# Reading the second up-projection tile of the first pair ahead of its convolution, and broadcasting the second norm's factors two steps of k sooner

## The chip, the cores and the metric

The kernel runs on one core of one Trainium2 chip. The metric is the device time of that core in microseconds. Its engines are TensorE (PE in the profile; PEld is its weight load), VectorE (DVE), ScalarE (ACT), GpSimd (POOL) and SyncE (SP), which here only issues DMAs.

## The reference

One inference step of a decoder layer, for a prompt group (1 x 512 tokens) and a sample group (8 sequences x 8 tokens) that share the weights. The kernel puts both side by side as 576 token columns. What matters here is the part behind the mixers:

```
x = x + concat(retention, attention) @ w_out          # 1024 x 1024
h = rmsnorm(x, norm2_w)                                # mean of squares over 1024, per token
ua, ub = split(h @ w_up, 2816)                         # 1024 x 5632
conv = conv_b + sum_j buf[:, j:j+T] * conv_w[j]        # buf: two saved rows, then ua; width 3
x = x + (silu(conv) * ub) @ w_down                     # 2816 x 1024
y = rmsnorm(x, normf_w)
```

Data are float32.

## The kernel before

**Tiling.** Activations lie transposed: features on the 128 partitions, the 576 tokens along the free axis. A *dense* tile is a [128 features x 576 tokens] product, accumulated in two PSUM banks as two halves of 288 columns (`d` tiles, from the pool `psd` with two buffers). Float32 precision is made of three products: each operand is split into a high part and a low part (rounded to float32r, and the remainder), and high x high, high x low, low x high are summed. One *step of k* is thus six matmuls of 288 columns, three weight parts by two halves; a tile over 1024 input features is eight steps. Weights come as raw blocks by SP (`wraw`, `wrawb`), ScalarE makes the high part (`whi`, line 289), VectorE the low part (`wlo`, line 296), half a block (four steps) at a time, some halves ahead of use.

**The feed-forward part.** The 2816 features are 22 blocks f of 128, in chunks f = 0..7, 8..15, 16..21; after each chunk comes its share of the down projection. For each f two results are needed, the branch that is convolved (`pa`) and the one that multiplies it (`pb`). The odd f, and f=0, make them as two dense tiles, one after the other (`up`, `up_post`). The even f from 2 on make both by a scheme with seven products instead of eight (`up_seven`, `post_seven`): a *slab* of 84 matmuls at line 1274 into banks `m`, whose weights and inputs are sums and differences of quarters (`ws`, and the tiles `T`, made in `out_post` from line 1213 on). The fourth quarter of a slab adds into the bank of the first, and so needs that bank's copy by ScalarE (line 1280) first.

**The norm.** The second norm's factor is a number per token. It is not multiplied into h; the up projection runs on the unscaled h, and the products are scaled as they are read out of PSUM, by `rstd_b`. `norm2` makes it: sums over the features by matmul (line 1159), a reciprocal root in small VectorE steps, and then `row_broadcast`, five transposes (line 415) which spread the factors over the partitions, and two copies (lines 416, 417). Nothing of f=0 can be read out before that.

**After the products of f=0** (`up_post`): line 1337 and 1338 read `pa` out into `ue` (scaled), ScalarE starts the convolution (line 1341), VectorE adds the two other taps (lines 1345, 1346), ScalarE takes the silu (line 1348), VectorE reads `pb` out as `g` (line 1353), multiplies both (`gated`, lines 1320, 1321), and ScalarE and VectorE split the result into `ghi` and `glo` (lines 1323, 1325), the inputs of the down projection.

**Order.** Every engine runs its own queue in the order in which the program issues it. A small planner, `Merge`, sets that order: each stage is a generator, and what it yields is an estimate in ns, first of the TensorE work just issued and then of the time until its next piece should be issued; `yield None` waits for a flag. TensorE's dense stream drives the planner's clock (738 per step of k). The numbers in the yields are thus due times that decide places in queues, not waits on the chip. A `d` tile takes over the buffer of an earlier one, and its first matmul waits for the last reader of that one.

Of the kernel before, what the change touches and what calls it, by code (L numbers as in the profile page):

```python
# [22 lines left out]
T = NP + NS  # L23
# [123 lines left out]
def decoder_step(ctx, tc, a):  # L147
    nc = tc.nc
    pe, dve, act, pool, sp = nc.tensor, nc.vector, nc.scalar, nc.gpsimd, nc.sync
# [208 lines left out]
    def tok(ps):  # L358
        return ps[:, C0:C0 + T]
# [27 lines left out]
    rstd_b = cst.tile([P, T], F32, name="rstd_b")  # L387
# [18 lines left out]
    def rstd_cols(dst, ss, n):  # L406
        dve.tensor_scalar(ss, ss, 1.0 / n, EPS, op0=OP.mult, op1=OP.add)
        rsqrt(dst, ss, stat[:, 35:40])

    def row_broadcast(dst, cols):  # L410
        p1, p2 = mtile(), mtile()
        for j in range(5):
            r, s = rows_of(j)
            ps = p1[:, s] if j < 4 else p2[:, :NS]
            pe.transpose(ps, cols[:r, j:j + 1].to_broadcast([r, P]), ident[:r, :r])
        dve.tensor_copy(dst[:, :NP], p1)
        dve.tensor_copy(dst[:, NP:], p2[:, :NS])
# [713 lines left out]
    def tmp(name):  # L1131
        return fp.tile([P, UE], F32, name=name, tag="tmp", bufs=6)
# [21 lines left out]
    def token_sums(dst, x):  # L1154
        dve.memset(dst, 1.0)
        ps = mtile()
        for j in range(5):
            r, s = rows_of(j)
            pe.matmul(ps[:r, j:j + 1], x[:, s], ones[:, 0:1], start=True, stop=True)
        dve.tensor_copy(dst[:, 0:4], ps[:, 0:4])  # L1160
        dve.tensor_copy(dst[:NS, 4:5], ps[:NS, 4:5])
# [14 lines left out]
    def norm2():  # L1176
        token_sums(ss2, acc)
        rstd_cols(stat[:, 20:25], ss2, D)
        yield 2200.0, 3700.0
        row_broadcast(rstd_b, stat[:, 20:25])  # L1180
        norm2_made.append(1)
        yield 550.0, 100.0
# [15 lines left out]
    def out_post(m, ps):  # L1198
# [15 lines left out]
        if last:  # L1214
            yield 0.0, 5000.0
            yield from norm2()
# [21 lines left out]
    def seqs(t, off, n):  # L1238
        return t[:, NP + 2:UE].rearrange("p (b t) -> p b t", b=B)[:, :, off:off + n]

    def by_seq(x):
        return x.rearrange("p (b t) -> p b t", b=B)

    def up(f, n, ghi, glo, made):
        if f in SEVEN:
            yield from up_seven(f, n, ghi, glo, made)
            return
        pa = dtile()
        yield from dense(pa, ("up", f), hhis, hlos, 0, KD, True, True, made=h_made)
        pb = dtile()  # L1250
        done = []
        mg.add(up_post(f, n, pa, pb, done, ghi, glo, made), None, 4000.0 if f == 0 else 0.0)
        yield from dense(pb, ("up", NF + f), hhis, hlos, 0, KD, True, True)
        done.append(1)
# [63 lines left out]
    def gated(f, n, g, c, ghi, glo, made):  # L1318

        dve.tensor_tensor(g[:, :NP], g[:, :NP], c[:, :NP], op=OP.mult)  # L1320
        dve.tensor_tensor(by_seq(g[:, NP:T]), by_seq(g[:, NP:T]), seqs(c, 0, TS), op=OP.mult)  # L1321
        yield 0.0, 1000.0
        act.copy(ghi[n], g[:, :T])  # L1323
        yield 0.0, 1500.0
        dve.tensor_sub(glo[n], g[:, :T], f32(ghi[n]))  # L1325
        made[n] = 1
        up_made.append(f)
        if f % 2 == 0:
            keep_rows()

    def up_post(f, n, pa, pb, done, ghi, glo, made):
        u = ues[f % 2]
        ya, L = tok(pa), UE - 2
        while not norm2_made or not cs_made:
            yield None
        pool.tensor_copy(seqs(u, 0, 2), by_seq(csT[:, f]))
        dve.tensor_mul(u[:, 2:NP + 2], ya[:, :NP], rstd_b[:, :NP])
        dve.tensor_mul(seqs(u, 2, TS), by_seq(ya[:, NP:]), by_seq(rstd_b[:, NP:]))  # L1338
        yield 0.0, 1800.0
        c = tmp("cv")  # L1340
        act.activation(c[:, :L], u[:, 0:L], AF.Identity, scale=convw[:, 0, f:f + 1], bias=convb[:, f:f + 1])
        pool.tensor_copy(cout[:, 0:2, f], u[:, NP:NP + 2])
        pool.tensor_copy(by_seq(cout[:, 2:, f]), seqs(u, TS, 2))
        yield 0.0, 1800.0
        dve.scalar_tensor_tensor(c[:, :L], u[:, 1:L + 1], convw[:, 1, f:f + 1], c[:, :L], op0=OP.mult, op1=OP.add)
        dve.scalar_tensor_tensor(c[:, :L], u[:, 2:L + 2], convw[:, 2, f:f + 1], c[:, :L], op0=OP.mult, op1=OP.add)
        yield 0.0, 1300.0
        act.activation(c[:, :L], c[:, :L], AF.Silu)
        while not done:
            yield None  # L1350
        yield 0.0, 1400.0
        g = tmp("g")
        dve.tensor_mul(g[:, :T], tok(pb), rstd_b)
        yield 0.0, 1000.0
        yield from gated(f, n, g, c, ghi, glo, made)

    def conv_state_out():
# [175 lines left out]
```

## Time and profile before

| | us |
|---|---|
| median of 3 runs | 824.35 |
| lowest and highest run | 824.2, 825.31 |
| profiled execution, own time | 825.07 |
| its span, first to last instruction | 823.3 |
| TensorE busy in the span | 796.0 (97%) |
| VectorE busy | 518.2 (63%) |
| ScalarE busy | 345.0 (42%) |
| mean granted clock of TensorE | 0.990 of full |

All the times in the rows further down are microseconds from the span's start; a row's second number is the length of the piece or instruction. `L341` is a line of the program, `d<-hhi,whi` says what is written from what, and brackets give the idle time of that engine just before, with what ended it. The second norm lies at 393 to 401 us, f=0 and f=1 up to 421, then slabs and dense pairs alternate up to 487, and the first chunk's down projection follows.

### The profile page before, as it was taken

To read this page: it belongs to the slowest core of one execution; us is meant where nothing else is said; L and a number is where in the kernel's file an instruction comes from. 1 tells how busy PE (TensorE), PEld (TensorE's weight loads), DVE (VectorE), ACT (ScalarE), POOL (GpSimd) and SP (SyncE) were. 2 spreads that over 40 slices of the span, in tenths; PEclk is the share of its full clock that TensorE was granted. 3 is DMA by queue.
4 is the path that set the end of the run, shared out by engine and by line. 5 is a ranking of instruction groups with operands and counts; after the bars stand their busy time and mean duration, and the time that the engine had idled before them with its cause. 6 is when DMAs were issued, how large, how long until landed. Compare 5 with 4: busy or idle time off the path is not lost.

```text
span 823.3 us, 16179 instructions
## 1 busy us (share of the span) xinstructions
PE 796.0 (97%) x6439; PEld 757.5 (92%) x6439; DVE 518.2 (63%) x1098; ACT 345.0 (42%) x691; POOL 99.0 (12%) x199
## 2 busy tenths in 40 slices
PE   7999999999999999999899999999999999999994
PEld 6999999887888888999799999999999999999994
DVE  5664555665646566787767875347878534778663
ACT  5423232454535567456334452124444312444522
POOL 1311202011110213022001100000110000110021
PEclk9999999999999999999989999999999999999997
DMA  9355653778887863427245554215545621544603
GB/s 268 110 171 140 191 178 96 187 208 220 224 246 207 224 172 103 122 87 251 77 153 180 180 179 152 79 53 179 180 135 174 205 77 52 180 136 147 214 1 115
DMA packets 179673, 128.68 MB, mean 156 GB/s; under 512 B 14849, under 2 KB 176273, under 8 KB 179086
## 3 DMA queue, kind: packets, MB, share of 16 engines
q1 hardware_dynamic: 178445, 93.75, 40.3%
q10 hardware_dynamic: 928, 33.63, 11.3%
q8 instruction: 51, 0.84, 0.4%
q0 software_dynamic: 224, 0.28, 0.1%
q14 instruction: 25, 0.20, 0.1%
HBM read 121.52 MB, written 39.66 MB: 196 GB/s over the span
## 4 chain that ended last, share of the span: by engine, by line
PE 83%; DVE 8%; ACT 3%; issue 3%; DMA 1%; POOL 0%; ACTq 0%; SPq 0%; DVEq 0%; POOLq 0%
PE d L341 52%; PE m L1274 11%; PE m L980 3%; PE d L546 2%; PE m L1025 2%; DVE wlo L296 1%; PE m L907 1%; PE d L990 1%; PE m L894 1%; PE m L593 1%; ACT whi L289 1%; PE px L505 1%; DVE blo L1325 1%; PE px L341 1%; PE m L763 1%
## 5 line engine op out<-in xcount | busy, mean ns | idle before, releaser
L341 PE MATMUL d<-bhi,whi 128*128 128x288 f32 x786 | 176.8, 306 | 2.9 <-ACT bhi L1323 1.7
L341 PE MATMUL d<-blo,whi 128*128 128x288 f32 x786 | 168.1, 295 | 0.8 <-DVE blo L1325 0.8
L341 PE MATMUL d<-bhi,wlo 128*128 128x288 f32 x786 | 168.1, 295 | 0.0
L341 PEld LDWEIGHTS d<-bhi,whi 128*128 128x128 f32 x786 | 124.6, 189 | 8.7 <-issue 3.1
L341 PEld LDWEIGHTS d<-blo,whi 128*128 128x128 f32 x786 | 126.0, 188 | 1.5 <-DVE blo L1325 1.5
L341 PEld LDWEIGHTS d<-bhi,wlo 128*128 128x128 f32 x786 | 126.2, 188 | 0.0
L296 DVE TENSOR_TENSOR wlo<-wraw,whi 128x512 fp32r<-128x512 f32 (+1 forms) x145 | 99.7, 705 | 39.5 <-ACT whi L289 39.3
L289 ACT ACTIVATE whi<-wraw 128x512 fp32r<-128x512 f32 (+1 forms) x145 | 87.3, 619 | 81.2 <-PE d L341 71.8
L341 PE MATMUL d<-hhi,whi 128*128 128x288 f32 x312 | 67.9, 299 | 4.4 <-DVE ue L1338 4.4
L341 PE MATMUL d<-hhi,wlo 128*128 128x288 f32 x312 | 67.7, 298 | 0.0
L341 PE MATMUL d<-hlo,whi 128*128 128x288 f32 x312 | 67.4, 298 | 0.0
L341 PEld LDWEIGHTS d<-hhi,whi 128*128 128x128 f32 x312 | 51.0, 192 | 4.9 <-issue 4.8
L341 PEld LDWEIGHTS d<-hlo,whi 128*128 128x128 f32 x312 | 50.8, 191 | 0.0
L341 PEld LDWEIGHTS d<-hhi,wlo 128*128 128x128 f32 x312 | 50.8, 191 | 0.0
L1274 PE MATMUL m<-T,whi 128*128 128x288 f32 x240 | 48.6, 295 | 0.0
L1389 DVE TENSOR_TENSOR xT<-d,xT 128x576 f32<-128x576 f32 x23 | 17.4, 757 | 40.7 <-PE d L341 40.7
L296 DVE TENSOR_TENSOR wlo<-wrawb,whi 128x512 fp32r<-128x512 f32 (+1 forms) x32 | 22.6, 713 | 28.7 <-ACT whi L289 28.7
L1274 PEld LDWEIGHTS m<-T,whi 128*128 128x128 f32 x240 | 38.4, 188 | 0.2 <-ACT ct L1280 0.2
L1274 PE MATMUL m<-T,wlo 128*128 128x288 f32 x120 | 35.5, 296 | 0.0
L1323 ACT CAST bhi<-g 128x576 fp32r<-128x576 f32 x22 | 14.8, 674 | 49.1 <-DVE g L1321 49.0
L888 POOL TENSOR_SCALAR s<-s,sc 128x128 f32<-128x128 f32 (+3 forms) x32 | 18.3, 579 | 140.4 <-DVE sc L886 125.8
L981 ACT COPY kt<-m 128x384 f32<-128x384 f32 x32 | 15.3, 478 | 39.3 <-PE m L980 37.2
(333 smaller groups left out, 1574.7 us busy)
## 6 DMA issues: line engine op xcount, KB each, us to landing
wraw<-in_w_up_dram SPq DMA_DIRECT2D x33, 512.0 KB, 3.7
wraw<-in_w_in_dram SPq DMA_DIRECT2D x26, 512.0 KB, 6.4
kc<-in_cache_win_k_dram SPq DMA_DIRECT2D x32, 256.0 KB, 3.5
vc<-in_cache_win_v_dram SPq DMA_DIRECT2D x32, 256.0 KB, 3.5
wraw<-in_w_down_dram SPq DMA_DIRECT2D x12, 512.0 KB, 3.5
wrawb<-in_w_up_dram SPq DMA_DIRECT2D x11, 512.0 KB
kc<-in_cache_win_k_dram SPq DMA_DIRECT2D x64, 64.0 KB, 3.3
vc<-in_cache_win_v_dram SPq DMA_DIRECT2D x64, 64.0 KB, 3.1
```

The costliest lines, as they stand in the source:

```text
L289: act.activation(split[j][0][:, :n], src, AF.Copy)
L296: dve.tensor_sub(split[j][1][:, :n], src, f32(split[j][0][:, :n]))
L341: pe.matmul(ps[:, C0 + s * H2:C0 + (s + 1) * H2], wt[:, x], b[k][:, s * H2:(s + 1) * H2], start=first and k == k0 and wt is hi and b is xh ...
L505: pe.transpose(ps[:, s], xn[:r, j, k * P:(k + 1) * P], ident[:r, :r])
L546: pe.matmul(ps[i][:, C0 + s * H2:C0 + (s + 1) * H2], wt[:, k % 4], x[k][:, s * H2:(s + 1) * H2], start=k == 0 and wt is hi and x is xhis, ...
L888: pool.tensor_scalar(s[:, :n], s[:, :n], c[:, 2:3], 1.0, op0=OP.mult, op1=OP.mult)
L980: pe.transpose(ps[:, j * P:(j + 1) * P], K[u, x][:, 3 * w + j], ident)
L981: (act.copy if w else dve.tensor_copy)(kt[:, w * 384:w * 384 + 384], ps[:, :384])
L1025: pe.matmul(ps[x * 32:(x + 1) * 32, :P], pt[:, j, x * 32:(x + 1) * 32], v, start=j == 0, stop=j == 6, tile_position=(0, x * 32))
L1274: pe.matmul(dst, wt[:, k], b[:, k], start=q in (0, 1, 2, 5) and k == 0 and wt is hi and b is xh, stop=k == 3 and wt is lo, skip_group_chec ...
L1323: act.copy(ghi[n], g[:, :T])
L1389: dve.tensor_add(xT[:, m], tok(ps), xT[:, m])
```

## The change

Two edits. In `norm2` the due time of the broadcast goes from 3700 to 2300 behind the small steps. In `up_post`, for f=0 alone, `g` is read out of `pb` before the two taps of the convolution on VectorE; this piece waits until all matmuls of `pb` are issued. For the other f nothing changes in the code.

```diff
     def norm2():
         token_sums(ss2, acc)
         rstd_cols(stat[:, 20:25], ss2, D)
-        yield 2200.0, 3700.0
+        yield 2200.0, 2300.0
         row_broadcast(rstd_b, stat[:, 20:25])
...
         pool.tensor_copy(by_seq(cout[:, 2:, f]), seqs(u, TS, 2))
+        g = None
+        if f == 0:
+            while not done:
+                yield None
+            yield 0.0, 500.0
+            g = tmp("g")
+            dve.tensor_mul(g[:, :T], tok(pb), rstd_b)
         yield 0.0, 1800.0
         dve.scalar_tensor_tensor(c[:, :L], u[:, 1:L + 1], convw[:, 1, f:f + 1], c[:, :L], op0=OP.mult, op1=OP.add)
...
         yield 0.0, 1400.0
-        g = tmp("g")
-        dve.tensor_mul(g[:, :T], tok(pb), rstd_b)
-        yield 0.0, 1000.0
+        if g is None:
+            g = tmp("g")
+            dve.tensor_mul(g[:, :T], tok(pb), rstd_b)
+            yield 0.0, 1000.0
         yield from gated(f, n, g, c, ghi, glo, made)
```

The lines behind the second edit get higher numbers in the changed kernel: 1345, 1346 and 1348 become 1352, 1353 and 1355, and the product g is line 1350 for f=0 and 1361 for the other dense f.

First place, TensorE's queue in the second tile of f=0 (`d_5123`), whose weights come as two halves (`whi_5026`, then `whi_5058`) of four steps each. Before:

```order
L341 MATMUL d_5123<-hhi_4457,wlo_5066 128x288 x2
L415 MATMUL m_5196<-ident_69,stat_74 128x128 x4
L415 MATMUL m_5197<-ident_69,stat_74 128x64
L341 MATMUL d_5123<-hhi_4457,whi_5058 128x288 x2
L341 MATMUL d_5123<-hlo_4458,whi_5058 128x288 x2
L341 MATMUL d_5123<-hhi_4457,wlo_5066 128x288 x2
L341 MATMUL d_5217<-hhi_4457,whi_5095 128x288 x2
```

And in the changed kernel, same queue and tile:

```order
L341 MATMUL d_5123<-hhi_4457,wlo_5034 128x288 x2
L341 MATMUL d_5123<-hhi_4457,whi_5058 128x288 x2
L341 MATMUL d_5123<-hlo_4458,whi_5058 128x288 x2
L341 MATMUL d_5123<-hhi_4457,wlo_5066 128x288 x2
L415 MATMUL m_5184<-ident_69,stat_74 128x128 x4
L415 MATMUL m_5185<-ident_69,stat_74 128x64
```

The transposes stood behind the third step of the second half, one step ahead of the first tile of f=1 (`d_5217`); now they stand behind its first step, three steps ahead.

Second place, TensorE's queue where the second tile of f=1 begins, with what its first matmul waits for. Before (`d_5217` and `d_5297` are the first and second tile of f=1):

```order
L341 MATMUL d_5217<-hhi_4457,wlob_5132 128x288 x2
L341 MATMUL d_5297<-hhi_4457,whi_5174 128x288 [waits DVE_49,PE_49,Activation_49]
L341 MATMUL d_5297<-hhi_4457,whi_5174 128x288
L341 MATMUL d_5297<-hlo_4458,whi_5174 128x288 x2
L341 MATMUL d_5297<-hhi_4457,wlo_5182 128x288 x2
```

In the changed kernel the two tiles are called `d_5225` and `d_5299`:

```order
L341 MATMUL d_5225<-hhi_4457,wlob_5132 128x288 x2
L341 MATMUL d_5299<-hhi_4457,whi_5174 128x288 [waits DVE_49,Activation_49]
L341 MATMUL d_5299<-hhi_4457,whi_5174 128x288
L341 MATMUL d_5299<-hlo_4458,whi_5174 128x288 x2
L341 MATMUL d_5299<-hhi_4457,wlo_5182 128x288 x2
```

The matmuls are the same; the first one's wait on TensorE itself (on the end of an earlier tile in the buffer that it takes over) is gone, a wait on VectorE and one on ScalarE stay.

Third place, the queues of VectorE and ScalarE from the T tiles to the convolution of f=1. On VectorE, the first piece of the difference (`ue_4467` belongs to f=0):

```order
 L1195 TENSOR_TENSOR T<-h,T 128x288
+L1350 TENSOR_TENSOR g<-d,rstd_b 128x576
+L1195 TENSOR_TENSOR T<-h,T 128x288
 L278 TENSOR_TENSOR ws<-ws,wraw 128x512
 L296 TENSOR_TENSOR wlo<-wraw,whi 128x512
-L1195 TENSOR_TENSOR T<-h,T 128x288
-L1345 SCALAR_TENSOR_TENSOR cv<-ue_4467,vec,cv 128x592
-L1346 SCALAR_TENSOR_TENSOR cv<-ue_4467,vec,cv 128x592
+L1352 SCALAR_TENSOR_TENSOR cv<-ue_4467,vec,cv 128x592
+L1353 SCALAR_TENSOR_TENSOR cv<-ue_4467,vec,cv 128x592
```

The read of g stood behind these rows; it now stands before the last T low half and before the convolution of f=0. A little further on the same queue (`ue_4469` belongs to f=1):

```order
 L1338 TENSOR_TENSOR ue_4469<-d,rstd_b 128x8x8
-L1353 TENSOR_TENSOR g<-d,rstd_b 128x576
 L1320 TENSOR_TENSOR g<-g,cv 128x512
 L1321 TENSOR_TENSOR g<-g,cv 128x64
 L270 TENSOR_TENSOR wraw<-wraw 128x512
 L296 TENSOR_TENSOR wlob<-wraw,whib 128x512
-L1345 SCALAR_TENSOR_TENSOR cv<-ue_4469,vec,cv 128x592
-L1346 SCALAR_TENSOR_TENSOR cv<-ue_4469,vec,cv 128x592
-L1325 TENSOR_TENSOR blo<-g,bhi 128x576
+L1325 TENSOR_TENSOR blo<-g,bhi 128x576
+L1352 SCALAR_TENSOR_TENSOR cv<-ue_4469,vec,cv 128x592
+L1353 SCALAR_TENSOR_TENSOR cv<-ue_4469,vec,cv 128x592
```

The low half of f=0's product (line 1325) has passed the convolution of f=1. ScalarE's queue over the same stretch, before:

```order
L289 ACTIVATE whi<-wrawb 128x512 x2
L1193 ACTIVATE T<-t 128x288 x2
L1341 ACTIVATE cv<-ue_4467,vec 128x592
L1193 ACTIVATE T<-h 128x288 x2
L289 ACTIVATE whi<-wraw 128x512
L1348 ACTIVATE cv<-cv 128x592
L289 ACTIVATE whi<-ws 128x512
L1341 ACTIVATE cv<-ue_4469,vec 128x592
L289 ACTIVATE whib<-wraw 128x512
L1323 CAST bhi<-g 128x576
```

And in the changed kernel:

```order
L289 ACTIVATE whi<-wrawb 128x512
L1193 ACTIVATE T<-t 128x288 x2
L1341 ACTIVATE cv<-ue_4467,vec 128x592
L289 ACTIVATE whi<-wrawb 128x512
L1193 ACTIVATE T<-h 128x288 x2
L289 ACTIVATE whi<-wraw 128x512
L1355 ACTIVATE cv<-cv 128x592
L289 ACTIVATE whi<-ws 128x512
L1323 CAST bhi<-g 128x576
L1341 ACTIVATE cv<-ue_4469,vec 128x592
L289 ACTIVATE whib<-wraw 128x512
```

One weight split has fallen behind the T tiles and the activation of f=0, and the cast of f=0's product (line 1323) has passed the activation of f=1 and the weight split behind it. The queues of GpSimd and SP hold the same instructions in the same order.

## Rows read from the trace of the kernel before

**Rows 1.** The waits of TensorE, 380 to 520: us in total, times, longest us.
```profile
PE d L341 <- DVE ue L1338: 4.4, 2, 3.9
```

**Rows 2.** Timeline of TensorE, 392 to 424: start, us, what, [idle before <-releaser].
```profile
399.47 0.80 PE L415 MATMUL m<-ident,stat 128*128 128x128 f32 x5
400.20 0.53 PE L341 MATMUL d<-hhi,whi 128*128 128x288 f32 x2
...
401.80 0.50 PE L341 MATMUL d<-hhi,whi 128*128 128x288 f32 x2 [0.55 <-DVE ue L1338]
...
412.26 0.82 PE L341 MATMUL d<-hhi,whi 128*128 128x288 f32 x2 [3.86 <-DVE ue L1338]
...
421.47 0.29 PE L1274 MATMUL m<-hhi,whi 128*128 128x288 f32 x1
```

**Rows 3.** Windows: length, busy by engine, granted clock, DMA share, GB/s.
```profile
225.00:235.00 10.00, 8.77 (x83) 8.12 (x85) 6.34 (x17) 5.16 (x12) 2.57 (x9) 1.00 0.83 255
412.30:418.20 5.90, 5.90 (x25) 5.90 (x26) 4.75 (x8) 2.21 (x4) 0.21 (x2) 0.50 0.93 325
432.00:445.00 13.00, 13.00 (x100) 13.00 (x99) 9.69 (x20) 6.14 (x11) 2.19 (x6) 1.00 0.51 161
```

**Rows 4.** Timeline of VectorE, 392 to 425.
```profile
396.97 0.17 DVE L400 SCALAR_TENSOR_TENSOR stat<-stat 128x5 f32<-128x5 f32 x1
...
400.11 0.69 DVE L416 COPY rstd_b<-m 128x512 f32<-128x512 f32 x1 [2.36 <-PE m L415]
...
405.76 0.46 DVE L1195 TENSOR_TENSOR T<-h,T 128x288 fp32r<-128x288 f32 x1 [0.57 <-ACT T L1193]
...
412.03 0.75 DVE L1353 TENSOR_TENSOR g<-d,rstd_b 128x576 f32<-128x576 f32 x1
...
415.62 0.83 DVE L1346 SCALAR_TENSOR_TENSOR cv<-ue,vec,cv 128x592 f32<-128x592 f32 x1
...
418.63 0.69 DVE L296 TENSOR_TENSOR wlo<-ws,whi 128x512 fp32r<-128x512 f32 x1 [1.51 <-ACT whi L289]
424.23 0.69 DVE L296 TENSOR_TENSOR wlo<-ws,whi 128x512 fp32r<-128x512 f32 x1 [4.90 <-ACT whi L289]
```

**Rows 5.** Timeline of ScalarE, 392 to 425.
```profile
402.90 0.87 ACT L1341 ACTIVATE cv<-ue,vec 128x592 f32<-128x592 f32 x1
...
417.97 0.63 ACT L289 ACTIVATE whi<-ws 128x512 fp32r<-128x512 f32 x1 [3.63 <-PE d L341]
...
423.26 0.40 ACT L1280 COPY ct<-m 128x288 f32<-128x288 f32 x1 [4.07 <-PE m L1274]
```

**Rows 6.** Timeline of VectorE at the convolutions of f=3, 5, 7, 11, 13.
```profile
444.84 0.69 DVE L296 TENSOR_TENSOR wlo<-wraw,whi 128x512 fp32r<-128x512 f32 x1 [1.44 <-ACT whi L289]
445.45 0.75 DVE L1325 TENSOR_TENSOR blo<-g,bhi 128x576 fp32r<-128x576 f32 x1
...
446.98 0.84 DVE L1346 SCALAR_TENSOR_TENSOR cv<-ue,vec,cv 128x592 f32<-128x592 f32 x1
...
471.83 0.84 DVE L1346 SCALAR_TENSOR_TENSOR cv<-ue,vec,cv 128x592 f32<-128x592 f32 x1
...
494.98 0.84 DVE L1346 SCALAR_TENSOR_TENSOR cv<-ue,vec,cv 128x592 f32<-128x592 f32 x1
...
594.98 0.83 DVE L1346 SCALAR_TENSOR_TENSOR cv<-ue,vec,cv 128x592 f32<-128x592 f32 x1
...
619.83 0.84 DVE L1346 SCALAR_TENSOR_TENSOR cv<-ue,vec,cv 128x592 f32<-128x592 f32 x1
```

**Rows 7.** Chain of waits, 470 to 505 and 545 to 630: start, us, what.
```profile
500.09 4.93 PE d L341 x35
...
545.54 11.14 PE m L1274 x84
556.68 12.70 PE d L341 x96
...
617.01 11.55 PE m L1274 x84
```

## Prediction

> **What bounds the kernel now.** I read three views for one question: where does TensorE stand still, and who lets it go on. The waits between 380 and 520 us name a single large one: matmuls of line 341 waited 4.4 us for VectorE's line 1338, in two pieces, the longer 3.9 us [rows 1]. The timeline of TensorE puts them at 401.80 and 412.26 us, each at the first matmul of a new d tile [rows 2]: first and second tile of f=1. A row calls line 1338 the releaser because the second tile of f=1 took over the buffer of the first tile of f=1, and had to wait until that tile was read. The windows add what the pause costs afterwards: in the 5.9 us behind it the granted clock was 0.50, the 1.2 GHz level, where other stretches show 1.00 [rows 3].
>
> The second thing to see is less plain. VectorE's conv step of the odd f (line 1346) ends the vector chain of a pair of f. It starts at 446.98 for f=3 and at 471.83 for f=5, and in the second chunk at 594.98 and 619.83: 24.85 us apart each time [rows 6]. TensorE's own period for such a pair is shorter: four slabs start between 545.54 and 617.01, so (617.01 - 545.54) / 3 = 23.82 us [rows 7]. So VectorE and ScalarE, handing work to each other, go round in 24.85 us by themselves, and TensorE gains about 1 us on them per pair. That shows in the slab at 617.01, which took 11.55 us where the one at 545.54 took 11.14 [rows 7]: there the lead of the vector side is used up. A busy TensorE in these stretches is no proof that it sets the time. The down projection of the first chunk starts at 500.09, only after the vector chain's last piece, 5.1 us after the conv of f=7 at 494.98 [rows 6, 7].
>
> From f=1 to f=3 the same conv step takes 446.98 - 415.62 = 31.36 us [rows 4, 6]: 6.51 more than 24.85. VectorE's idle rows there give 1.51 and 4.90, together 6.41 [rows 4]; both times for ScalarE, which itself sat idle 3.63 and 4.07 us for TensorE [rows 5]. This is how the pause at 412 reaches the end of the chunk.
>
> **The change, step by step.** Durations are from the profiled execution: span 823.3 us, own time 825.07, which is 0.72 above the median of the runs, 824.35. One step of k is six matmuls; 96 of them, a pair of tiles, take 12.70 us [rows 7], so a step takes 0.79 and a tile 6.35.
>
> *Transposes two steps sooner.* They stood at 399.47 [rows 2], and come to 399.47 - 1.59 = 397.88. Their input is ready: the last step on the factors starts at 396.97 and takes 0.17 [rows 4]. Line 416 follows at 400.11 - 1.59 = 398.52, and so does everything behind it on VectorE. The count of matmuls is the same; TensorE's wait at 401.80 goes, since the buffer's reader is now done by about 400.1 and TensorE arrives at about 401.0 (400.20 plus one step). Gain there 0.8.
>
> *g of f=0 read ahead.* The same product of 0.75 us [rows 4], neither added nor removed, now stands before the last of the T tiles' low halves and before the conv. On ScalarE one weight split (0.63) falls behind the activation of line 1341 (0.87) [rows 5]. Its end becomes 402.90 - 1.59 + 0.87 + 0.63 = 402.81; the vector queue would otherwise come to its low half about 0.5 us before. Bounds for this wait are 0 and 0.87; I take 0.5. The T low half that stood at 405.76 [rows 4] then starts at 405.76 - 1.59 + 0.5 = 404.67, and g ends 0.46 + 0.75 later, near 405.9. TensorE reaches the second tile of f=1 at 401.0 + 6.35 = 407.4. So 1.5 us are to spare, the tile starts without a wait, and with no pause the clock has no reason to fall. Before, the tile started at 412.26, 4.1 after 401.80 + 6.35; and it took until 421.47, 9.21 instead of 6.35 [rows 2]. TensorE therefore comes to the first slab at about 413.7: 0.8 + 4.1 + 2.9 = 7.7 us sooner.
>
> *What the vector side makes of it.* From line 416 to the conv step of f=1 it took 415.62 - 400.11 = 15.51 us. Three things are added. The 0.5 above. Then the low half of the product g (line 1325, 0.75), which now stands before f=1's conv and stood behind it. And the order ScalarE now has, in which cast and activation precede a weight split that VectorE wants: the same order stands before f=3's conv, and there VectorE sat idle 1.44 [rows 6]. Together 15.51 + 0.5 + 0.75 + 1.44 = 18.20, from 398.52: the conv of f=1 starts at 416.72, which is 1.1 us *later* than before. But the 6.51 us of waiting after it go, because TensorE, 7.7 sooner, is no longer what is waited for. f=3's conv comes to 416.72 + 24.85 = 441.57 instead of 446.98: 5.41 sooner. From there both kernels run the same instructions in the same order; f=5, f=7, and the down projection keep the 5.4.
>
> Seen from TensorE it is the same sum: 7.7 gained, then about 0.3 us given back in the first slab and 24.85 - 23.82 = 1.03 in each of the two others, where it now waits for the copy of its first product bank, which stands behind the odd f's silu on ScalarE: 5.3.
>
> The moved steps issue no DMA. SP's weight loads hang on VectorE's low halves and keep their order; none of VectorE's listed waits in this stretch of the trace is for a transfer, and I cost them at nothing. If that cover failed, the loads would come late in both kernels, at the same point of the vector chain.
>
> Sum: 825.07 - 5.4 = 819.7 for a profiled execution, and **819.0 us** against the median.
>
> **Rivals.**
>
> *All of the 7.7 us stay: 816.7.* For it: TensorE and its weight loads are busy 13.00 of 13 us in 432 to 445, VectorE 9.69 [rows 3]. The Trainium skill (Perfetto Trace Analysis, "Identifying the Most-Contended Engine") says that the engine with the highest occupancy is the one whose gaps are to be closed, TensorE being judged by its weight loads; by that rule the gap's whole 7.7 would come back. Against it stands the 24.85 us period, shown twice, against TensorE's 23.82.
>
> *The second tile of f=1 still takes the first one's buffer: 824.0.* Then the early read frees nothing. Its releaser is then still line 1338 of f=1, which comes 1.59 - 0.5 - 0.75 = 0.34 sooner, and pause and half clock remain. For it: the profile names line 1338 for both waits. Against it: the first matmul of that tile loses its wait on TensorE's own earlier tile in the changed order.
>
> *Slower: the clock falls at the slabs, 827.6.* TensorE will now stop for about 1 us in the slabs of f=4 and f=6 and for less in that of f=2. If such stops brought the granted clock to 0.50, each would cost what the one at 412 cost, 9.21 - 6.35 = 2.86; three make 8.6, and from the second on (5.7) the gain is gone. Against it: in 225 to 235 us TensorE was busy 8.77 of 10 us, at a clock of 1.00 [rows 3]. The Trainium skill (TensorE: Matmul & The Clock Gate, "A second HAM failure mode: psum-queue depth-cycling") tells of a kernel whose frequent short idles between matmul groups made the clock swing; this row does not bear it out here.
>
> **How the numbers follow.** Forecast 0.84, all of it 0.07, buffer kept 0.05, clock 0.02, something else that cancels it 0.02. A difference of 0.2% is 1.65 us, about what a measurement tells from none. Faster by more: the first two cases, 0.91. Within: the kept buffer and most of the rest, 0.06. Slower: 0.03. The range: at the low end the full 7.7 (816.7) is partly let in; at the high end the 1.51 us idle before 418.63 might not go, which leaves 3.9 (820.5), and the three runs of before lie up to 0.96 from their median. That makes 816.9 to 821.1.
>
> **What would show it.** Right: line 415 near 397.9; no idle of TensorE before either tile of f=1; no half clock near 412; first slab near 413.7; the conv of f=1 near 416.7, a little later than before; f=3's near 441.6; stops of about 1 us in the slabs of f=4 and f=6; down projection near 494.7. Wrong: a releaser "line 1338" before the second tile of f=1, a clock of 0.50 in a slab, or f=3's conv more than 26 us after f=1's.

## The result and the profile after

The changed kernel takes 820.06 us (median of five runs, 819.24 to 820.61), the kernel before on the same chip 824.97 (five runs, 824.20 to 825.45). The ratio is 0.9941, with an interval of 0.9927 to 0.9955: 4.9 us less, between 3.7 and 6.0. The forecast was 819.0, which meant 5.4 less. Its direction and its path held; one term was too large, and the kernels below show which.

The profiled execution of after took 820.61 us, its span 818.6. Before comparing times in two traces one has to line them up. The second norm's sums (line 1159) are the last thing on TensorE that the change can't touch, and they already differ. First before, then after, both the timeline of TensorE:

```profile
393.52 1.16 PE L1159 MATMUL m<-small,acc 128*128 128x1 f32 x10
```

```profile
394.79 1.16 PE L1159 MATMUL m<-small,acc 128*128 128x1 f32 x10
399.15 0.80 PE L415 MATMUL m<-ident,stat 128*128 128x128 f32 x5
402.36 0.43 PE L341 MATMUL d<-hhi,whi 128*128 128x288 f32 x2
408.73 0.42 PE L341 MATMUL d<-hhi,whi 128*128 128x288 f32 x2
415.07 0.29 PE L1274 MATMUL m<-hhi,whi 128*128 128x288 f32 x1
```

The profiled execution of after comes to that point 1.27 us later. The instructions up to there are the same, and the difference is there within the first 22 us of the span: the same matmuls of line 505 start at 20.02 us in before and at 21.38 in after. So 1.27 is taken off each time of after: line 415 at 397.88, the first slab at 413.80, where before had 399.47 and 421.47 [rows 2]. There is no idle time before either tile of f=1 (402.36 and 408.73), where before had 0.55 and 3.86 [rows 2]. The waits of TensorE between 380 and 520 us (us in total, times, longest) no longer name line 1338 [rows 1]:

```profile
PE m L1274 <- ACT ct L1280: 1.1, 2, 0.6
PE d L341 <- ACT bhi L1323: 0.4, 1, 0.4
PE d L341 <- DVE blo L1325: 0.3, 1, 0.3
```

The windows (length, busy time by engine, granted clock, DMA share, GB/s), one over the tiles of f=1, two over the slabs in which TensorE waits, all show the full clock, where before fell to 0.50 [rows 3]:

```profile
399.00:415.00 16.00, 16.00 (x122) 15.76 (x121) 12.88 (x27) 5.91 (x11) 2.45 (x6) 1.00 0.12 34
437.00:450.00 13.00, 12.45 (x93) 12.07 (x92) 9.63 (x19) 6.88 (x14) 1.72 (x3) 1.00 0.62 204
462.00:474.00 12.00, 11.43 (x86) 11.20 (x86) 8.68 (x17) 6.03 (x12) 1.72 (x3) 1.00 0.65 218
```

VectorE's timeline answers to [rows 4, 6]:

```profile
399.79 0.69 DVE L416 COPY rstd_b<-m 128x512 f32<-128x512 f32 x1 [0.78 <-PE m L415]
...
406.38 0.75 DVE L1350 TENSOR_TENSOR g<-d,rstd_b 128x576 f32<-128x576 f32 x1
...
415.81 0.69 DVE L296 TENSOR_TENSOR wlob<-wraw,whib 128x512 fp32r<-128x512 f32 x1 [1.44 <-ACT whib L289]
416.42 0.75 DVE L1325 TENSOR_TENSOR blo<-g,bhi 128x576 fp32r<-128x576 f32 x1
417.95 0.84 DVE L1353 SCALAR_TENSOR_TENSOR cv<-ue,vec,cv 128x592 f32<-128x592 f32 x1
...
442.81 0.83 DVE L1353 SCALAR_TENSOR_TENSOR cv<-ue,vec,cv 128x592 f32<-128x592 f32 x1
...
467.66 0.83 DVE L1353 SCALAR_TENSOR_TENSOR cv<-ue,vec,cv 128x592 f32<-128x592 f32 x1
```

The product g is read at 406.38 (line 1350), well ahead of TensorE's 408.73. The conv of f=1 is *later* than before, 416.68 after the 1.27 are off, against 415.62 [rows 4], with the 1.44 us idle and line 1325 now ahead of it. f=3's comes at 441.54 against 446.98 [rows 6], and the odd f's conv steps lie 24.86 and 24.85 us apart. Where TensorE stands in the slabs, the timelines of ScalarE and of TensorE show:

```profile
443.68 0.70 ACT L1355 ACTIVATE cv<-cv 128x592 f32<-128x592 f32 x1 [2.52 <-DVE cv L1353]
444.28 0.38 ACT L1280 COPY ct<-m 128x288 f32<-128x288 f32 x1
```

```profile
444.71 0.53 PE L1274 MATMUL m<-T,whi 128*128 128x288 f32 x2 [0.55 <-ACT ct L1280]
```

VectorE's conv at 442.81, ScalarE's silu at 443.68, its copy at 444.28, TensorE at 444.71: a chain from one engine to the next. The next slab repeats it (0.57 us at 469.57). From its first matmul to that of the dense tile behind it, the slab itself is longer by more than this stop:

```profile
439.22 0.29 PE L1274 MATMUL m<-hhi,whi 128*128 128x288 f32 x1
...
451.38 0.43 PE L341 MATMUL d<-hhi,whi 128*128 128x288 f32 x2
```

That is 12.16 us, where a slab without waits took 11.14 [rows 7]. The slab behind it (464.07 to 476.24) takes 12.17 and the first one (415.07 to 426.52) 11.45. The down projection starts in the chain of waits at 495.91, which is 494.64 lined up, behind the vector side's last piece:

```profile
495.10 0.77 DVE blo L1325
495.91 4.17 PE d L341 x30
```

### The profile page after: what moved, and what is told of

The parts are those of the page before. It is cut to its first block, busy times and chain, and to the rows that moved or that the text cites. A ratio compares the mean times of both kernels' runs of the same rounds, so it can differ in the third digit from the quotient of the medians.

```text
span 818.6 us, 16178 instructions
## 1 busy us (share of the span) xinstructions
PE 794.7 (97%) x6439; PEld 755.2 (92%) x6439; DVE 518.2 (63%) x1098; ACT 344.8 (42%) x691; POOL 100.0 (12%) x199
## 4 chain that ended last, share of the span: by engine, by line
PE 81%; DVE 10%; ACT 4%; issue 3%; DMA 1%; ACTq 0%; POOL 0%; SPq 0%; DVEq 0%; POOLq 0%
PE d L341 51%; PE m L1274 10%; PE m L980 3%; PE d L546 2%; DVE wlo L296 2%; PE m L1025 2%; PE m L907 1%; PE d L990 1%; PE m L894 1%; ACT whi L289 1%; PE m L593 1%; DVE blo L1325 1%; PE px L505 1%; DVE g L1320 1%; PE px L341 1%
```

## The experiments

Times in the table are counted from each execution's own line 1159. "f=3's conv" is VectorE's step for that f, "chunk 2" the first slab of the second chunk, "end" the last instruction.

| kernel | median us | ratio to before (95%) | first slab | f=3's conv | chunk 2 | end |
|---|---|---|---|---|---|---|
| before, the execution forecast from | 824.35 (this run 825.07) | – | 27.95 | 53.46 | 151.86 | 429.77 |
| before, execution a | 824.09 (one run) | – | 26.69 | 52.21 | 150.59 | 428.76 |
| before, execution b | 823.98 (one run) | – | 26.56 | 52.07 | 150.47 | 428.53 |
| before, execution c | 823.79 (one run) | – | 26.58 | 52.09 | 150.49 | 428.41 |
| after | 820.06 | 0.9941 (0.9927 to 0.9955) | 20.29 | 48.02 | 146.25 | 423.86 |
| broadcast alone | 819.22 | 0.9938 (0.9925 to 0.9952) | 22.10 | 47.62 | 146.03 | 423.69 |
| early read alone | 820.53 | 0.9950 (0.9937 to 0.9962) | 21.07 | 48.38 | 146.79 | 424.42 |
| before, stop filled | 823.22 | 0.9979 (0.9969 to 0.9990) | 25.18 | 50.70 | 149.10 | 427.00 |
| before, later cast | 820.89 | 0.9957 (0.9945 to 0.9970) | 26.69 | 51.40 | 149.21 | 423.83 |
| after, later cast | 812.87 | 0.9857 (0.9835 to 0.9878) | 20.29 | 46.36 | 142.79 | 417.41 |
| broadcast and later cast | 814.41 | 0.9877 (0.9861 to 0.9894) | 22.10 | 46.81 | 144.63 | 419.28 |

**Broadcast alone.** Before, with one line changed:

```diff
-        yield 2200.0, 3700.0
+        yield 2200.0, 2300.0
```

Expected: 

> The broadcast's due time alone (3700 to 2300), g read where it was before. Theory (the chain of VectorE and ScalarE, 24.85 us per pair of f, sets the end of the first chunk, and a pair's d buffer is the price of entry): with the broadcast two steps sooner the queues put g of f=0 ahead of the read of f=1's first tile by themselves, so the second tile of f=1 takes over the other buffer; TensorE pauses there about 1.9 us instead of 3.9. f=1's conv stays near its old place (0.3 later), f=3's conv comes 5.9 sooner if the granted clock stays at 1.00 after the shorter pause: about 5.9 us faster than before, 0.5 better than both edits together. If the clock falls to 0.50 as before, 2.8 of it is lost: about 3.1 faster. Rival (only the early read of g frees the buffer, the broadcast just shifts the queue by two steps): 1.6 faster.

It came to 819.22, as good as both edits together, and the rival's 1.6 us is out. The early read is therefore not needed to free the buffer. Timelines of TensorE and VectorE:

```profile
409.00 0.50 PE L341 MATMUL d<-hhi,whi 128*128 128x288 f32 x2 [1.58 <-DVE g L1353]
```

```profile
408.11 0.75 DVE L1353 TENSOR_TENSOR g<-d,rstd_b 128x576 f32<-128x576 f32 x1
...
409.98 0.68 DVE L1337 TENSOR_TENSOR ue<-d,rstd_b 128x512 f32<-128x512 f32 x1
```

Once line 416 is earlier, g of f=0 stands ahead of f=1's first read in VectorE's queue even at its old place in the code, so that the second tile of f=1 takes g's buffer. g is only late: TensorE stops for 1.58 us (expected 1.9), and the window over that stop keeps the full clock:

```profile
395.00:412.00 17.00, 15.42 (x116) 14.97 (x115) 14.89 (x37) 5.14 (x10) 2.27 (x4) 1.00 0.18 52
```

Its first slab is 1.8 us later than that of after, and yet f=3's conv is 0.4 sooner: in these stretches TensorE's lead is worth nothing.

**Early read alone.** After, with `2200.0, 3700.0` put back, so that the broadcast stands where it stood.

Expected: 

> The early read of g alone; the broadcast keeps its due time of 3700. Theory: TensorE keeps its 0.55 us wait at the first tile of f=1, the second tile starts without a wait and at full clock; f=1's conv 1.5 later than before, f=3's 4.8 sooner: about 4.8 us faster than before, nearly all of the change. Rival (the two edits add up, and the broadcast is worth the 1.6 us that it moves): about 3.3 to 3.8 faster.

820.53. What is left at line 341 in the waits is the first tile's stop:

```profile
PE d L341 <- DVE ue L1338: 0.5, 1, 0.5
```

Either edit alone removes the long stop, and either alone frees the buffer. They do not add: 5.5 us alone (824.68 - 819.22), 4.2 alone (824.68 - 820.53) and 4.9 together, with intervals that overlap. The 4.2, between 3.1 and 5.2, doesn't by itself tell the expected 4.8 from the rival's 3.3 to 3.8; the 5.5 of the broadcast alone, for which the rival had 1.6, does. Lined up, both edits together are 0.4 to 0.6 us ahead of the early read alone.

**The stop filled.** Before, with 30 matmuls more, of which nothing is read, ahead of the second tile of f=1. The buffer comes free when it did; only the idle TensorE, and with it the half clock, goes.

```diff
-        pb = dtile()
+        pb = ([pe.matmul(fm, hhi[:, 0, :P], hhis[0][:, :H2], start=True, stop=True) for fm in [mtile()[:, :H2]] for _ in range(30)] if f == 1 else 0, dtile())[1]
```

Expected: 

> The kernel before, with 30 extra matmuls of 288 columns into an unused bank between the two tiles of f=1 (about 4.0 us at full clock), whose results nobody reads: they fill the pause, so that TensorE is busy where it stood still, and the second tile starts when it did before, about 412.3. This takes the clock by itself. Theory: the granted clock stays at 1.00, the second tile takes 6.4 instead of 9.2 us, the vector side waits less in the first slab, and the kernel is 2.8 us faster. Rival (the vector chain sets the time and does not wait for TensorE there, or the clock falls for another reason): within 0.5 us of before.

The timeline and a window, with the full clock where before had 0.50. The second tile starts 18.76 us after line 1159, in before 18.74:

```profile
409.17 4.11 PE L1250 MATMUL m<-hhi 128*128 128x288 f32 x30
```

```profile
413.00:419.50 6.50, 6.50 (x51) 6.39 (x50) 5.60 (x10) 3.41 (x5) 0.45 (x3) 1.00 0.87 313
```

The mechanism is as expected, and half the size: 1.5 us by the medians (824.68 - 823.22), between 0.8 and 2.6, where the profile of before says 2.9. So the kernel before was profiled three more times.

**Before, three more executions.** No edit.

Expected, of the first: 

> The kernel before, unchanged, a further look. In its first profile the granted clock was 0.50 for 6.8 us after the pause; in the kernel before with the cast change the same pause of 3.9 us was followed by 3.4 us. Theory (how long the half clock lasts varies from execution to execution; the forecast took its cost from one execution with the long one): some looks show 3.4 and a slab start 1.4 to 1.7 us earlier, measured from the second norm's sums, others 6.8. Rival (it is 6.8 in this kernel always, and what the change is short of the forecast was lost elsewhere): 6.8 in every look.

In execution b, the timeline of TensorE and two windows behind the stop:

```profile
412.38 0.82 PE L341 MATMUL d<-hhi,whi 128*128 128x288 f32 x2 [3.87 <-DVE ue L1338]
...
420.20 0.29 PE L1274 MATMUL m<-hhi,whi 128*128 128x288 f32 x1
```

```profile
412.10:415.50 3.40, 3.12 (x13) 3.15 (x14) 3.37 (x8) 2.08 (x3) 0.46 (x3) 0.50 0.65 217
415.50:418.90 3.40, 3.40 (x28) 3.40 (x27) 2.41 (x4) 1.22 (x2) 0.00 (x0) 1.00 1.00 366
```

The stop is the same (3.87 against 3.86 us), but the half clock ends after 3.41 us. In the execution that the forecast rests on it lasted 6.83, all through the window of [rows 3]:

```profile
411.62:415.03 3.41, 2.77 (x11) 2.80 (x12) 3.38 (x8) 2.08 (x3) 0.46 (x3) 0.50 0.35 120
415.03:418.45 3.42, 3.42 (x16) 3.42 (x16) 2.06 (x3) 0.48 (x1) 0.00 (x0) 0.50 1.37 479
```

In execution b the tile takes 420.20 - 412.38 = 7.82 us, not 9.21, so the half clock costs 1.5, not 2.9. The other two show 3.41 as well; none of the three shows the long one that the theory expected in some.

**The loop of VectorE and ScalarE.** The forecast says that their round of 24.85 us, longer than TensorE's 23.82, swallows part of the gain. Then a shorter round must let it through. In `gated`, the cast that makes the high half of the product g is put off by 1200 in the step's due time:

```diff
-        yield 0.0, 1000.0
+        yield 0.0, 2200.0
```

First in before.

Expected: 

> The kernel before, with one due time changed in the common end of all f (the cast of the product, line 1323, due 2200 instead of 1000 after the multiplication), so that ScalarE makes the weight split that VectorE wants ahead of the cast. Nothing of the change itself. Theory: this shortens the round of VectorE and ScalarE from 24.85 us per pair to TensorE's 23.8, in all three chunks; the waits at the fourth slab and at the start of each down projection go: about 5 us faster than before, with the pause at 408 to 412 and the half clock still there. The change on top of it should then be worth TensorE's full 7.7 us. Rival (the 24.85 us come from something else, such as the weight loads): no change, or slower, since the product comes later.

820.89, 3.8 us less by the medians: in the right direction, and smaller than expected. Lined up, the end lies 4.6 to 4.9 us ahead of executions a, b and c, about what was expected; why the medians show only 3.8 was not settled. This execution, too, had the short half clock (0.50 in the first 3.4 us, 1.00 in the next):

```profile
413.40:416.80 3.40, 3.38 (x14) 3.40 (x15) 3.33 (x7) 2.05 (x3) 0.27 (x2) 0.50 0.02 5
416.80:420.20 3.40, 3.40 (x28) 3.40 (x27) 2.18 (x3) 1.28 (x2) 0.00 (x0) 1.00 1.27 405
```

What the loop cost before is gone: the fourth slab of the second chunk, 11.55 us in before [rows 7], is, in the chain of waits,

```profile
615.51 11.12 PE m L1274 x84
```

Then the same line in after.

Expected: 

> The changed kernel with the same due time of the cast (2200 for 1000) that the kernel before was given in the run named e6_cast_before. Theory: once the round of VectorE and ScalarE is no longer than TensorE's, nothing of the change is given back in the slabs; no stops of TensorE there, none at the down projections of the first two chunks. In traces lined up at the second norm's sums (line 1159) the second chunk's first slab is 7 to 7.7 us ahead of the cast change alone, or 5.6 to 6 if the half clock in that kernel's execution lasts 3.4 us and not 6.8. The time: 820.9 less 6 to 7, 814 to 815. Rival (the change is worth about 5 us whatever the vector side does): 816.

812.87, lower than expected and the best of all kernels run: 1.4% under before. On top of the later cast the change is worth 820.89 - 812.87 = 8.0 us by the medians, where it was worth 4.9 without it. That is more than TensorE's lead can account for: lined up, after with the later cast is 6.4 us ahead of before with it at the first slab, at chunk 2 (149.21 - 142.79) and at the end (423.83 - 417.41), so the whole lead is kept, where without the later cast 4.6 to 4.9 of 6.3 to 6.4 are left at the end. Where the other 1.6 of the medians come from was not settled. The expectation had 7 to 7.7, or 5.6 to 6 for the short half clock. From the chain of waits and from VectorE's timeline:

```profile
414.65 11.11 PE m L1274 x84
425.76 12.70 PE d L341 x96
438.46 11.14 PE m L1274 x84
449.60 12.69 PE d L341 x96
462.29 11.12 PE m L1274 x84
473.41 26.67 PE d L341 x201
```

```profile
440.57 0.83 DVE L1353 SCALAR_TENSOR_TENSOR cv<-ue,vec,cv 128x592 f32<-128x592 f32 x1
...
464.45 0.83 DVE L1353 SCALAR_TENSOR_TENSOR cv<-ue,vec,cv 128x592 f32<-128x592 f32 x1
```

The conv steps are 23.88 us apart instead of 24.85, close to TensorE's own 11.12 + 12.70 = 23.82, and the chain stays on TensorE from the first slab into the down projection without a break. In the order of ScalarE's instructions the activation of line 1341 for f=1, 3 and 5 now stands ahead of the cast of the product before, and in each slab one weight split more does (two instead of one). The expectations spoke of the weight splits; which of these moves shortens the round was not tried apart.

**Broadcast and later cast.** Before with both one-line edits, g not moved. Does the early read matter once the loop is short?

Expected: 

> The broadcast's due time alone (as in e1_bcast) together with the later cast (as in e5_cast_after); g read where it was. It asks what the early read of g is worth where the vector side is no longer the slower one. Theory: TensorE's pause of 1.6 us before the second tile of f=1 is then not absorbed by anything and stays to the end, so this kernel is 1.6 to 1.9 us slower than with the early read: about 814.6, where the same step cost nothing without the later cast (819.22 against 820.06). Rival (the early read is worth nothing, since the broadcast alone already frees the buffer in time): 812.9, as with it.

814.41 against 812.87, beside runs of before at 824.62 and 824.50. The intervals of the ratios overlap a little, but the runs do not (814.18 to 815.09 and 812.36 to 814.05), and the 1.5 us between them is about the size of the one stop left, in the waits between 380 and 780 us:

```profile
PE d L341 <- DVE g L1353: 1.6, 1, 1.6
```

In the lined-up times its lead stays open from the first slab (22.10 against 20.29) to chunk 2 (144.63 against 142.79) and the end (419.28 against 417.41). So the early read is worth 1.5 to 1.9 us where TensorE sets the time, and nothing that can be measured where the loop sets it (820.06 with it, 819.22 without).

## Why the prediction was right, and where it was not

*Transposes two steps sooner: right.* 397.88 lined up, forecast 397.9; the stop of 0.55 us at the first tile is gone.

*g read ahead: right as to the time, incomplete as to the reason.* The tile starts without a wait, and g is through 1.6 us before TensorE needs it (406.38 + 0.75 against 408.73; forecast 1.5). But the forecast gave the early read the credit for the buffer. Broadcast alone has the same exchange of buffers, with a short stop, and so has the early read alone, without one. The rival "buffer kept", 824.0, is out for both edits.

*TensorE 7.7 us sooner at the first slab: right against that execution, too large for the kernel.* The step "9.21 instead of 6.35", the clock term of 2.9, was mis-sized. It came from one execution with 6.83 us of half clock; four others (executions a, b and c of before, and before with the later cast) had 3.41, and the filled stop moved the medians by 1.5. Against executions a, b and c the first slab of after is 6.3 to 6.4 us sooner, not 7.7.

*The vector side: right in each step.* The conv of f=1 came at 416.68 (forecast 416.72), f=3's at 441.54 (441.57), the down projection at 494.64 (494.7), and ScalarE's order cost the 1.44 us idle that was borrowed from f=3. That the loop gives gain back is shown twice: broadcast alone comes 1.8 us later to the first slab and loses nothing by it, and the shorter loop raises what is left of TensorE's lead at the end from 4.6 to 4.9 us to 6.4. From TensorE's side the forecast gave back 0.3, 1.03 and 1.03 us in the three slabs; they are 0.31, 1.02 and 1.03 longer than 11.14. Only 0.55 and 0.57 of that shows as a stop, where the forecast looked for about 1; what the rest is was not settled.

*The sum.* At the conv of f=3 after is 5.44 us ahead of the execution that was forecast from (forecast 5.41), but only 4.05 to 4.19 ahead of executions a, b and c. The constant of 0.72 by which the sum went over to the median did not carry this: the runs of before lay within about 1 us, though in the profiled one the tile behind the stop took 1.4 us longer. With 7.82 in place of 9.21 the same sum gives 5.41 - 1.39 = 4.0 us less, or 820.3; that the forecast came within 0.5 us of the measured 4.9 is thus in part luck. At the start of chunk 2 the lead over a, b and c is 4.2 to 4.3, at the end 4.6 to 4.9, near the 4.9 of the medians. Where the last 0.3 to 0.6 come from was not settled.

*The rivals.* All of 7.7 kept is refuted for this loop: the conv steps stay 24.85 us apart. The Trainium skill (Perfetto Trace Analysis, "Identifying the Most-Contended Engine") calls the engine with the highest occupancy the most contended, judges TensorE by MFU (its share of peak arithmetic) and weight loads, and has that engine optimized first; that its gap then comes back whole is what the forecast read from it. The trace disagrees with that reading: in 437 to 450 us the weight loads are busy 12.07 of 13 us and VectorE 9.63, and yet TensorE waits for ScalarE, which waited for VectorE. The rival with the clock falling at the slabs is refuted by the two windows at 1.00, and a stop of 1.58 us did not bring it down either. The swing of which the Trainium skill tells (TensorE: Matmul & The Clock Gate, "A second HAM failure mode: psum-queue depth-cycling") shows in none of these rows.

## What to carry to other kernels

A busy engine is not always the one that sets the time: compare the period of a repeated line on each engine, and price a removed stop only up to the point where the longer period takes over; with that loop shortened, 6.4 us of the change's lead reached the end, and without 4.6 to 4.9 (by the medians 8.0 and 4.9). A cost of the clock read from one execution is one draw; look at two or three more before it goes into a sum. Line up two traces at the last instruction that the change can't touch, and look at what each part of a change does alone: here one of its two edits was enough, as long as the loop set the time.

## What was not expected of the hardware

After the same stop of TensorE (3.86 and 3.87 us) the clock stood at half for 6.83 us in one execution of the same program and for 3.41 in three others; stops of 1.58 us and of about 0.55 us left it at full. The profiled executions of before and after, with the same instructions up to the second norm, came to it 1.27 us apart, all of it from the first 22 us. In them pairs of matmuls of 288 columns that first took 0.68 to 0.85 us come down to 0.42 to 0.54 from 12.4 us on in before and from 14.9 in after. The four executions of before reached the second norm within 0.12 us of each other, those of the other kernels at 393.12 to 394.79 us; whether a difference belongs to the execution or to the program was not tried.
